# A hybrid decoder layer: chunk levels of gated linear attention by running products of decays on 64x64 quarters, and the gate's product in one fp32r pass

## The chip, the cores and the metric

The kernel runs on one core of a Trainium2 chip. The metric is the device time of one execution in microseconds (us), the median of several. The engines are named as in the profile: PE (TensorE matmuls), PEld (its weight loads, which overlap them), DVE (VectorE), ACT (ScalarE), POOL (GpSimd) and SP (SyncE, which here issues nearly all DMAs).

## The reference

One layer: x (1, 256, 1024) float32; RMSNorm, one input projection, softmax attention with 8 heads of 64 (one block of 256 keys, so plain causal attention per query block of 128), gated linear attention with 4 heads (key width 64, value width 128), an output projection, then a gated feed-forward block with a short convolution. The change touches the gated linear attention alone:

```python
log_a = jax.nn.log_sigmoid((gate_lr @ w_gate_up[l] + b_gate[l]).astype(jnp.float32)) / GLA_GATE_TAU

def gla_attention(q, k, v, log_a):
    """S_t = diag(alpha_t) S_{t-1} + k_t^T v_t ;  o_t = q_t S_t."""
    ...
    qc = to_chunks(q * (dk ** -0.5))
    kc, vc = to_chunks(k), to_chunks(v)
    G = jnp.cumsum(to_chunks(log_a), axis=3)
    ...
        diff = G_[:, :, :, None, :] - G_[:, :, None, :, :]
        decay = jnp.exp(jnp.where(causal[None, None, :, :, None], diff, -jnp.inf))
        A = jnp.einsum('bhtd,bhsd,bhtsd->bhts', q_, k_, decay)
```

So A[t, s] is the sum over d of q[t, d] k[s, d] times the product of the decays of the positions s+1 to t; gate_lr has 16 columns (RANK).

## The kernel before

All matrices stand transposed, 128 features by tokens. Products of the large projections are made in fp32r with both factors split into a high and a low part: `mm3` (L108 to L111) issues three matmuls, high by high, high by low, low by high. ACT makes the high part of each weight piece (`split_hi`, L92), DVE the low part (`split_lo`, L95), half a slot of 2048 columns at a time, ahead of its use; SP loads the next slot when one is free.

The attention runs in 64 steps q (L613 to L659). Steps 0 to 7 project the gated attention's q, k and the gate's 16 columns; 8 to 23 project the softmax heads' q and k (twelve 256-column matmuls a step); 24 to 47 project v, the gated attention's v and its output gate (six 512-column matmuls a step); 48 to 63 are the output projection, and the feed-forward block follows. A table `plan` (L540 to L592) names what else is emitted at the start of each step: `on(q, f)`. PE's order is exactly that of the code. The instructions of ACT and DVE are ordered by a scheduler, with `tc.high_priority()` for the softmax's maxima and exponentials (`m_softmax1`) and for `m_pt`; each engine then works its list in order.

PSUM: four banks `acc` for the projections, and four banks `att`, taken in turn by everything else. A fifth `att` waits until the first is released by its last reader.

The gated attention, before: `g_evac` copies the projection out (step 10), `g_transpose_lr` and `g_transpose` turn it (steps 10, 11), `g_gate_mm` (L297, step 12) multiplies the 16 gate columns in plain float32, which the profile records as two matmuls each; `g_gate` makes the log decay, `g_scan` the running sum Gc over each 128 tokens. The lower triangle of each 128x128 block is then made level by level. For a level with block length b in 32, 16, 8, 4, 2, 1, 64 (`LEVELS`), `lvl_a` subtracts Gc at the pivots and takes exp, `lvl_b` multiplies k and q by it into `kt` and `qt`, `lvl_c` makes the scores on PE, and `lvl_d_` copies the wanted ones under a mask into `ATd` (for 64, a plain copy into `AT`). `qt` holds the two heads of a pair side by side with zeros in the other head's rows, so that a matmul has 128 rows of k, 64 columns of stationary data and 64 moving columns (two heads by 32). The block of tokens 128 to 255 against 0 to 127 comes from `l128_a`, `l128_b`, `l128_c`.

The softmax heads come in pairs pr = 0 to 3: `m_scores(pr)` (step 30, 33, 36, 39) takes two banks, one a head, and multiplies 128 queries by 128 and by 256 keys; `m_softmax1` takes the maxima on DVE (L495) and the exponentials on ACT (L500); `m_pt` turns the weights (L515) and `m_av` multiplies by v (L527, L528). The level matmuls stand at steps 25, 27, 30, 33, 36, 38 and 41, the last block's at 44; in steps 30, 33 and 36 `lvl_c` is emitted right before `m_scores`.

Of the kernel before, what the change touches and what calls it, by code (L numbers as in the profile page):

```python
# [27 lines left out]
LEVELS = [32, 16, 8, 4, 2, 1, 64]  # L28
# [6 lines left out]
def trunk_kernel(ctx: ExitStack, tc: tile.TileContext, xT_d, wG_d, w5_d, wo_d, up_d, dn_d,  # L35
                 par_d, gla_g_d, fin_g_d, wgu_d, cos_d, sin_d, causal_d, lvl_d, ident_d, out_d):
    nc = tc.nc
    V, A, T, DMA = nc.vector, nc.scalar, nc.tensor, nc.sync
# [169 lines left out]
    lrT = at.tile([RANK, S], F32, name="lrT")  # L208
    kts = [at.tile([128, 512], F32, name=f"kt{i}") for i in range(2)]
    qts = [at.tile([128, 4, 2, 64], F32, name=f"qt{i}") for i in range(2)]  # L210
    qt128 = at.tile([128, 2, 2, 128], F32, name="qt128")
    resets = at.tile([128, 512], F32, name="y", bufs=2)
    nc.gpsimd.memset(resets, 1.0)
    nc.gpsimd.memset(resets.rearrange("p (n t) -> p n t", t=128)[:, :, 0:1], 0.0)
    for i in range(2):
        nc.gpsimd.memset(kts[i], 0.0)
        nc.gpsimd.memset(qts[i], 0.0)
    nc.gpsimd.memset(qt128, 0.0)
    nc.gpsimd.memset(AT[64:128, :, 0:64], 0.0)
    mqT = at.tile([128, 4, S], F32, name="mqT")  # L220
# [45 lines left out]

    def g_transpose_lr():
        p = att()
        for tt in range(2):
            T.transpose(p[:RANK, tt * 128:(tt + 1) * 128], gqk[:, tt, 256:272], ident)  # L270
        A.activation(lrT, p[:RANK, :S], AF.Copy)
# [22 lines left out]
    def g_gate_mm():  # L294
        p = att()
        for pr in range(2):
            T.matmul(p[:, pr * S:(pr + 1) * S], wgu[:, pr * 128:(pr + 1) * 128], lrT,  # L297
                     start=True, stop=True)
# [15 lines left out]
    def g_scan():  # L314
        la = at.tile([128, 512], F32, name="d", bufs=2)
        V.tensor_sub(la, st["mn"], st["ln"])
        V.tensor_tensor_scan(Gc, resets, la, 0.0, op0=ALU.mult, op1=ALU.add)

    lv = {}

    def lvl_a(l):
        b = LEVELS[l]
        d = at.tile([128, 512], F32, name="d", bufs=2)
        e = at.tile([128, 512], F32, name="e", bufs=2)
        dv = d.rearrange("p (n two b) -> p n two b", two=2, b=b)
# [4 lines left out]
        V.tensor_sub(dv[:, :, 0, :], pb, gvw[:, :, 0, :])  # L330
        V.tensor_sub(dv[:, :, 1, :], gvw[:, :, 1, :], pb)
        A.activation(e, d, AF.Exp, scale=1.0 / TAU)
        lv[l] = e

    def lvl_b(l):
        b = LEVELS[l]
        e = lv[l]
        kt, qt = kts[l % 2], qts[l % 2]

        def blk(x):  # L340
            return x.rearrange("p (n two b) -> p n two b", two=2, b=b)

        gk_ = gkT.rearrange("p a t -> p (a t)")
        gq_ = gqT.rearrange("p a t -> p (a t)")
        V.tensor_mul(blk(kt)[:, :, 0, :], blk(gk_)[:, :, 0, :], blk(e)[:, :, 0, :])  # L345
        for h in range(2):
            ps = slice(64 * h, 64 * h + 64)
            o = qt[ps, :, h, :].rearrange("p g (n b) -> p g n b", b=b)
            q_ = gq_[ps].rearrange("p (g n two b) -> p g n two b", g=4, two=2, b=b)[:, :, :, 1, :]
            e_ = e[ps].rearrange("p (g n two b) -> p g n two b", g=4, two=2, b=b)[:, :, :, 1, :]  # L350
            V.tensor_mul(o, q_, e_)  # L351

    def lvl_c(l):
        kt, qt = kts[l % 2], qts[l % 2]
        p = att()
        if LEVELS[l] == 64:
            for g in range(4):
                T.matmul(p[0:64, g * 128:(g + 1) * 128], kt[:, g * 128:g * 128 + 64],
                         qt[:, g].rearrange("p h t -> p (h t)"), start=True, stop=True)
        else:  # L360
            for g in range(4):
                for j in range(2):
                    T.matmul(p[64 * j:64 * j + 64, g * 64:(g + 1) * 64],
                             kt[:, g * 128 + 64 * j:g * 128 + 64 * j + 64],
                             qt[:, g, :, 32 * j:32 * j + 32], start=True, stop=True)
        st["lv", l] = p

    def lvl_d_(l):
        b = LEVELS[l]
        p = st["lv", l]  # L370
# [6 lines left out]
        V.copy_predicated(o, m, p[:, :256].rearrange("p (i n b) -> p i n b", i=8, b=b))  # L377
# [5 lines left out]
    def l128_a():  # L383
        d = at.tile([128, 2, 128], F32, name="d", bufs=2)
        e = at.tile([128, 2, 2, 128], F32, name="e", bufs=2)
        G4 = Gc.rearrange("p (a b t) -> p a b t", a=2, b=2)
        V.tensor_sub(d, G4[:, :, 0, 127:128].to_broadcast([128, 2, 128]), G4[:, :, 0, :])
        A.activation(e[:, 0], d, AF.Exp, scale=1.0 / TAU)
        A.activation(e[:, 1], G4[:, :, 1, :], AF.Exp, scale=1.0 / TAU)
        lv["128"] = e  # L390

    def l128_b():
        e = lv["128"]
        kt = kts[1].rearrange("p (a t) -> p a t", a=4)
        V.tensor_mul(kt[:, 0:2], gkT[:, :, 0:128], e[:, 0])
        for h in range(2):
            ps = slice(64 * h, 64 * h + 64)
            V.tensor_mul(qt128[ps, :, h, :], gqT[ps, :, 128:256], e[ps, 1])

    def l128_c():  # L400
        p = att()
        for pr in range(2):
            T.matmul(p[:, pr * 256:(pr + 1) * 256], kts[1][:, pr * 128:(pr + 1) * 128],
                     qt128[:, pr].rearrange("p h t -> p (h t)"), start=True, stop=True)
        A.activation(AT01.rearrange("p a t -> p (a t)"), p, AF.Copy)
# [74 lines left out]
    def m_scores(pr):  # L480

        for hh in range(2):
            st["s", 2 * pr + hh] = att()
        for c0, c1 in ((0, 128), (128, 384)):
            for hh in range(2):
                ps = slice(64 * hh, 64 * hh + 64)
                T.matmul(st["s", 2 * pr + hh][:, c0:c1], mqT[ps, pr, c0:c0 + 128], mkT[ps, pr, 0:c1 - c0],
                         start=True, stop=True)
# [74 lines left out]
    on(14, g_scan)  # L563
    for l in range(7):
        b = 21 + 11 * l // 4
        on(b, lvl_a, l)
        on(b + 1, lvl_b, l)
        on(b + 4, lvl_c, l)
        on(b + 5, lvl_d_, l)
    on(b + 5, lvl_join)  # L570
    on(39, l128_a)
    on(42, l128_b)
    on(44, l128_c)
# [457 lines left out]
```

## Time and profile before

| | us |
|---|---|
| median of three runs | 316.96 (316.83 to 317.05) |
| the profiled execution's own time | 317.14 |
| its span | 315.4 |
| PE busy, share of the span | 97% |
| DVE busy, share | 80% |
| ACT busy, share | 65% |
| granted PE clock, mean | 0.996 |

A busy engine is one that executes an instruction; PE's matmuls are pipelined and their ends are modelled, so what a matmul costs is read from the start of one row to the start of the next, not from its duration. The prediction works with such differences. In the views, `x16` after a group is the number of instruction records in it, and a bracket names the idle time before it and what ended that.

### The profile page before, as it was taken

What the parts mean: (1) busy time and instruction counts of PE and PEld (TensorE: products, weight loads), DVE (VectorE), ACT (ScalarE), POOL (GpSimd) and SP (SyncE); (2) the same over time, 40 slices, a digit from 0 to 9 for tenths busy, and PEclk for the clock granted to TensorE, in tenths of its full rate; (3) what the DMA queues carried; (4) which work ended last, traced back from release to release, by engine and by line L of the source; (5) the groups of instructions that cost most, each with busy time, mean ns of one, the idle gap of its engine ahead of it and who ended that gap; (6) DMA issues with size and microseconds to landing.
All of it is one profiled execution on the core that took longest, in us unless ns stands there. A gap on an engine that the chain in (4) does not pass through costs nothing.

```text
span 315.4 us, 5840 instructions
## 1 busy us (share of the span) xinstructions
PE 306.6 (97%) x2296; PEld 283.1 (90%) x2296; DVE 252.9 (80%) x472; ACT 203.8 (65%) x370; POOL 3.9 (1%) x17
## 2 busy tenths in 40 slices
PE   7899999999999999999999999999999999999992
PEld 6899997776888999999999999999999999999982
DVE  3887999999647677999999988877777777776643
ACT  5878989497858478367676556666665555544362
POOL 4000000000000000000000000000000000000000
PEclk9999999999999999999999999999999999999998
DMA  7999533342361525496555664545555622120003
GB/s 199 374 413 411 201 135 133 133 150 120 135 219 50 178 90 200 157 380 268 200 202 200 225 220 177 195 185 202 201 202 200 262 72 69 67 69 0 2 0 135
DMA packets 12444, 55.40 MB, mean 176 GB/s; under 512 B 1392, under 2 KB 3200, under 8 KB 8064
## 3 DMA queue, kind: packets, MB, share of 16 engines
q1 hardware_dynamic: 12272, 54.76, 47.2%
q8 instruction: 18, 0.29, 0.3%
q10 hardware_dynamic: 144, 0.26, 0.2%
q14 instruction: 10, 0.08, 0.1%
HBM read 53.97 MB, written 1.05 MB: 174 GB/s over the span
## 4 chain that ended last, share of the span: by engine, by line
PE 79%; DVE 9%; ACT 5%; issue 2%; DMA 2%; SPq 1%; DVEq 0%; ACTq 0%
PE att L109 14%; PE att L111 14%; PE att L110 14%; PE acc L110 11%; PE acc L109 10%; PE acc L111 10%; DVE lo L95 2%; DMA xg<-in_xT 2%; ACT qs L466 1%; DVE qt L351 1%; DVE att L495 1%; ACT hi L92 1%; PE att L527 1%; DVE ATd L377 1%; DVE kt L345 1%
## 5 line engine op out<-in xcount | busy, mean ns | idle before, releaser
L92 ACT ACTIVATE hi<-raw 128x1024 fp32r<-128x1024 f32 (+3 forms) x84 | 80.1, 971 | 50.9 <-PE att L110 43.2
L95 DVE TENSOR_TENSOR lo<-raw,hi 128x1024 fp32r<-128x1024 f32 (+3 forms) x86 | 93.7, 1098 | 13.3 <-ACT hi L92 13.2
L109 PE MATMUL att<-hh,hi 128*128 128x256 f32 x352 | 98.5, 280 | 0.0
L111 PE MATMUL att<-hh,lo 128*128 128x256 f32 x352 | 98.4, 279 | 0.0
L110 PE MATMUL att<-hl,hi 128*128 128x256 f32 x352 | 98.3, 279 | 0.0
L109 PEld LDWEIGHTS att<-hh,hi 128*128 128x128 f32 x352 | 66.2, 188 | 0.0
L111 PEld LDWEIGHTS att<-hh,lo 128*128 128x128 f32 x352 | 66.2, 188 | 0.0
L110 PEld LDWEIGHTS att<-hl,hi 128*128 128x128 f32 x352 | 66.2, 188 | 0.0
L757 DVE SCALAR_TENSOR_TENSOR c<-us,par,c 128x256 f32<-128x256 f32 x88 | 40.7, 482 | 4.1 <-ACT c L749 2.5
L749 ACT ACTIVATE c<-us,par 128x256 f32<-128x256 f32 x44 | 24.0, 591 | 21.5 <-DVE us L739 16.0
L111 PE MATMUL acc<-dhi,gl 128*128 128x512 f32 (+1 forms) x88 | 32.3, 367 | 0.0
L110 PE MATMUL acc<-dlo,gh 128*128 128x512 f32 (+1 forms) x88 | 32.2, 366 | 0.0
L109 PE MATMUL acc<-dhi,gh 128*128 128x512 f32 (+1 forms) x88 | 31.8, 361 | 0.0
L696 DVE TENSOR_TENSOR dlo<-draw,dhi 128x1024 fp32r<-128x1024 f32 x22 | 26.6, 1218 | 0.0
L739 DVE TENSOR_TENSOR us<-att,rb 128x512 f32<-128x512 f32 x20 | 13.8, 688 | 15.9 <-PE att L111 15.9
L109 PE MATMUL acc<-hi,ah 128*128 128x512 f32 (+1 forms) x64 | 25.6, 399 | 0.7 <-ACT hi L92 0.7
L110 PE MATMUL acc<-lo,ah 128*128 128x512 f32 (+1 forms) x64 | 24.2, 378 | 0.7 <-DVE lo L95 0.7
L111 PE MATMUL acc<-hi,al 128*128 128x512 f32 (+1 forms) x64 | 23.7, 371 | 0.0
L691 ACT ACTIVATE dhi<-draw 128x1024 fp32r<-128x1024 f32 x22 | 23.1, 1050 | 0.0
L110 PEld LDWEIGHTS acc<-dlo,gh 128*128 128x128 f32 x88 | 16.5, 188 | 3.0
L109 PEld LDWEIGHTS acc<-dhi,gh 128*128 128x128 f32 x88 | 16.6, 188 | 2.9
L111 PEld LDWEIGHTS acc<-dhi,gl 128*128 128x128 f32 x88 | 16.5, 188 | 2.6
(191 smaller groups left out, 528.9 us busy)
## 6 DMA issues: line engine op xcount, KB each, us to landing
raw<-in_up SPq DMA_DIRECT2D x22, 1024.0 KB, 4.8
draw<-in_dn SPq DMA_DIRECT2D x22, 512.0 KB, 5.7
raw<-in_w SPq DMA_DIRECT2D x8, 1024.0 KB, 7.3
raw<-in_wo SPq DMA_DIRECT2D x4, 1024.0 KB, 4.8
raw<-in_w SPq DMA_DIRECT2D x4, 512.0 KB, 8.1
raw<-in_wG SPq DMA_DIRECT2D x2, 528.0 KB, 7.3
raw<-in_wG SPq DMA_DIRECT2D x3, 264.0 KB, 4.0
xg<-in_xT SPq DMA_DIRECT2D x2, 256.0 KB, 6.4
```

Of the source, the lines that this page charges most:

```text
L92: A.activation(self.hi[:, a:b], self.raw[:, a:b], AF.Copy)
L95: V.tensor_sub(self.lo[:, a:b], self.raw[:, a:b], self.hi[:, a:b])
L109: T.matmul(out, sh, mh, start=first, stop=False, **kw)
L110: T.matmul(out, sh, ml, start=False, stop=False, **kw)
L111: T.matmul(out, sl, mh, start=False, stop=last, **kw)
L345: V.tensor_mul(blk(kt)[:, :, 0, :], blk(gk_)[:, :, 0, :], blk(e)[:, :, 0, :])
L351: V.tensor_mul(o, q_, e_)
L691: A.activation(hi, downs[i][0], AF.Copy)
L696: V.tensor_sub(lo, d, hi)
L739: V.tensor_tensor(u[:, :, 2:], upo[i][2].rearrange("p (a t) -> p a t", a=2), rb[:, None, :].to_broadcast([128, 2, S]), op=ALU.mult)
L749: A.activation(cv[i][:, a], u[:, a, 2:], AF.Identity, bias=par[:, P_CB + m:P_CB + m + 1], scale=par[:, P_CW + 2 * 2 * NP + m:P_CW + 2 * 2 ...
L757: V.scalar_tensor_tensor(c[:, a], u[:, a, w:w + S], par[:, wc:wc + 1], c[:, a], op0=ALU.mult, op1=ALU.add)
```

## The change

Three things are edited.

The gate's product: the 16 gate columns are split into high and low parts on DVE (`g_lr_split`) and stacked, so is its weight (`g_wgs`, two small copies on ACT and two subtractions on DVE), and `g_gate_mm` becomes one fp32r matmul with 128 rows for each pair of heads. The weight's load `wgu` moves from step 4 to step 1 in SP's list.

The levels: there is no running sum any more. `g_decay` takes the decay itself, `dec[0] = exp(la)`, and the levels run from small to large, b = 1, 2, 4, 8, 16, 32, each on the result of the one before: `lvl_u` multiplies the second half of each block of q by the running decay, the first half of k by its own, both in place, and multiplies neighbouring decays into a table of half the length. `lvl_c` no longer has zeros: each matmul has 64 rows (one head), 64 stationary and 32 moving columns, one quarter of the array, and the two heads go to two banks. The 64 level and the last 128x128 block are made together in `lvl_last`, also by quarters. What is written in place may not be overwritten before the matmuls of the level before have read it, so `lvl_u(l)` waits for the burst of level l-1.

The places: levels 0 and 1 go in one burst at step 24; levels 2 to 5 are emitted inside `m_scores`, in columns 384 to 511 of the two score banks, at steps 30, 33, 36 and 40 (the last pair was at 39), and the scores themselves are cut into quarters. `lvl_last` stands at step 44, its copies at 45. The fourth `m_av` moves from step 47 to 48.

```diff
-LEVELS = [32, 16, 8, 4, 2, 1, 64]
+LEVELS = [1, 2, 4, 8, 16, 32]
...
+    def g_wgs():
+        with tc.high_priority():
+            for i in range(2):
+                A.activation(wgs[32 * i:32 * i + RANK], wgu, AF.Copy)
+            for i in range(2, 4):
+                V.tensor_sub(wgs[32 * i:32 * i + RANK], wgu, wgs[0:RANK])
+
+    def g_lr_split():
+        with tc.high_priority():
+            lr = gqk[:, :, None, 256:272].to_broadcast([128, 2, 2, RANK])
+            l4 = lrs.rearrange("p a (n two z) r -> p a n two z r", two=2, z=2)[:, :, :, :, 0]
+            V.tensor_copy(l4[:, :, :, 0], lr)
+            V.tensor_sub(l4[:, :, :, 1], lr, l4[:, :, :, 0])
...
     def g_gate_mm():
         p = att()
         for pr in range(2):
-            T.matmul(p[:, pr * S:(pr + 1) * S], wgu[:, pr * 128:(pr + 1) * 128], lrT,
+            T.matmul(p[:, pr * S:(pr + 1) * S], wgs[:, pr * 128:(pr + 1) * 128], lrT,
                      start=True, stop=True)
...
-        V.tensor_tensor_scan(Gc, resets, la, 0.0, op0=ALU.mult, op1=ALU.add)
+        A.activation(dec[0], la, AF.Exp, scale=1.0 / TAU)
...
+    def lvl_u(l):
...
+        V.tensor_mul(two(gqf, c)[:, :, 1], q, dc[:, :, 0].to_broadcast([128, n, c]))
+        V.tensor_mul(two(gkf, c)[:, :, 0], two(gkf, c)[:, :, 0], dc[:, :, 1].to_broadcast([128, n, c]))
+        V.tensor_mul(dec[l], dc[:, :, 0, 0], dc[:, :, 1, 0])
...
+    def lvl_c(l, p, c):
         b = LEVELS[l]
...
+        for g in range(4):
+            for j in range(2):
+                for h in range(2):
+                    ps = slice(64 * h, 64 * h + 64)
+                    a = g * 128 + 64 * j
+                    q = q1[ps, a // 2:a // 2 + 32] if l == 0 else two(gqf[ps, a:a + 64], b)[:, :, 1]
+                    k = gk1.rearrange("p a t -> p (a t)") if l == 0 else gkf
+                    T.matmul(p[h][64 * j:64 * j + 64, c + 32 * g:c + 32 * g + 32], k[ps, a:a + 64], q,
+                             start=True, stop=True)
...
+    def lvl_last():
+
+        p = [att() for _ in range(2)]
+        for g in range(4):
+            for h in range(2):
+                ps = slice(64 * h, 64 * h + 64)
+                T.matmul(p[h][0:64, g * 64:(g + 1) * 64], gkf[ps, g * 128:g * 128 + 64],
+                         gqf[ps, g * 128 + 64:(g + 1) * 128], start=True, stop=True)
+        for pr in range(2):
+            for t, q in enumerate((gqT[:, pr, 128:192], q128[:, pr])):
+                for j, k in enumerate((k128[:, pr], gkT[:, pr, 64:128])):
+                    for h in range(2):
+                        ps = slice(64 * h, 64 * h + 64)
+                        c = 256 + pr * 128 + 64 * t
+                        T.matmul(p[h][64 * j:64 * j + 64, c:c + 64], k[ps], q[ps], start=True, stop=True)
...
     def m_scores(pr):
 
+        p = [att() for _ in range(2)]
+        lvl_c(pr + 2, p, 384)
+        for c0, c1 in ((0, 128), (128, 384)):
+            for j in range(2):
+                for hh in range(2):
+                    ps = slice(64 * hh, 64 * hh + 64)
+                    a = c0 + 64 * j
+                    T.matmul(p[hh][64 * j:64 * j + 64, c0:c1], mqT[ps, pr, a:a + 64], mkT[ps, pr, 0:c1 - c0],
+                             start=True, stop=True)
...
     for h in range(HM):
-        b = 30 + 3 * h // 2
+        b = (30, 33, 36, 40)[h // 2] + h % 2
         if h % 2 == 0:
             on(b, m_scores, h // 2)
+            on(b + 1, lvl_d_, 2 + h // 2)
...
+            on(b + 2, *((lvl_u, 3 + h // 2) if h < 6 else (lvl_u64,)))
```

Where the instructions stand now is shown at three places.

PE at step 36, where the third pair of softmax heads gets its scores. Before, with L363 as `lvl_c`, L487 as `m_scores` and L109 to L111 as the first product of the projection behind it:

```order
L363 MATMUL att<-qt_130,kt_128 64x64 x8
L487 MATMUL att<-mkT,mqT 128x128 x2
L487 MATMUL att<-mkT,mqT 128x256 x2
L109 MATMUL acc<-hi,ah 128x512
L110 MATMUL acc<-lo,ah 128x512
L111 MATMUL acc<-hi,al 128x512
```

Now, on PE at the same step, with L377 as `lvl_c` and L506 as `m_scores`:

```order
L377 MATMUL att<-gqT,gkT 64x32 x16
L506 MATMUL att<-mkT,mqT 64x128 x4
L506 MATMUL att<-mkT,mqT 64x256 x4
L109 MATMUL acc<-hi,ah 128x512
L110 MATMUL acc<-lo,ah 128x512
L111 MATMUL acc<-hi,al 128x512
```

The order of the three groups is kept, with twice the matmuls of half the width; the level's matmuls had a bank of their own and now go alternately to the two banks of the scores.

DVE ahead of the maxima of heads 2 and 3 (the pair of step 33). Before, with L508 and L506 of the softmax of heads 0 and 1, L345 and L351 as `lvl_b`, L377 as `lvl_d_` and L495 as the first maximum:

```order
L508 TENSOR_SCALAR pe<-pe,mx 128x256
L345 TENSOR_TENSOR kt_128<-gkT,e 128x128x2
L351 TENSOR_TENSOR qt_130<-gqT,e 64x4x64 x2
L506 RECIPROCAL mx<-mx 128x2
L377 COPY_PREDICATED ATd<-lvl,att 128x64x4
L495 ISA att,mx<-att,causal 128x128
```

Now, on DVE ahead of the same maxima, with L527 and L529 of the softmax of head 1, L352 and L353 as `lvl_u`, L388 as `lvl_d_` and L516 as the first maximum:

```order
L527 RECIPROCAL mx<-mx 128x2
L529 TENSOR_SCALAR pe<-pe,mx 128x256
L352 TENSOR_TENSOR gqT<-gqT,dec_128 128x32x8
L353 TENSOR_TENSOR gkT<-gkT,dec_128 128x32x8
L388 COPY_PREDICATED ATd<-lvl,att 128x4x4x8 x2
L516 ISA att,mx<-att,causal 128x128
```

Two products stand where three stood, two masked copies of half the size where one stood, and the whole softmax of head 1 is now ahead of them.

DVE behind those maxima, up to the two scalings L497 that ACT's exponentials of head 2 and of head 3 wait for. Before (L95 is a low part of a weight, L330 and L331 are `lvl_a`):

```order
L495 ISA mx 128x1
L497 TENSOR_SCALAR mx<-mx 128x2
L508 TENSOR_SCALAR pe<-pe,mx 128x256
L497 TENSOR_SCALAR mx<-mx 128x2
L95 TENSOR_TENSOR lo<-raw,hi 128x1024
L330 TENSOR_TENSOR d<-Gc 128x256
L331 TENSOR_TENSOR d<-Gc 128x256
L506 RECIPROCAL mx<-mx 128x2 x2
```

Now, on DVE at the same place, with L518 as the scaling:

```order
L516 ISA mx 128x1
L518 TENSOR_SCALAR mx<-mx 128x2
L95 TENSOR_TENSOR lo<-raw,hi 128x1024
L518 TENSOR_SCALAR mx<-mx 128x2
L527 RECIPROCAL mx<-mx 128x2
L95 TENSOR_TENSOR lo<-raw,hi 128x1024
L529 TENSOR_SCALAR pe<-pe,mx 128x256
```

A low part of 1024 columns now stands between the scaling of head 2 and that of head 3, where a short scaling of weights stood.

More of the change, by code (lines that the diff above doesn't have):

```diff
@@ L207, in trunk_kernel @@
     AT01 = at.tile([128, 4, 128], F32, name="AT01")
[L208 to L218, printed above, removed]
+    wgs = at.tile([128, 256], F32R, name="wgs")
+    lrs = at.tile([128, 2, 8, RANK], F32R, name="lrs")
+    lrT = at.tile([128, S], F32R, name="lrT")
     nc.gpsimd.memset(AT[64:128, :, 0:64], 0.0)
+    nc.gpsimd.memset(wgs.bitcast(F32), 0.0)
+    nc.gpsimd.memset(lrs.bitcast(F32), 0.0)
     mqT = at.tile([128, 4, S], F32, name="mqT")
@@ L280, in g_transpose @@
         A.activation(dst.rearrange("p a t -> p (a t)"), p, AF.Copy, scale=sc)
+        if which:
+            A.activation(gk1.rearrange("p a t -> p (a t)"), p, AF.Copy)
     def g_diag():
@@ L335, in lvl_b @@
-    def lvl_b(l):
-        b = LEVELS[l]
[L337 to L366, printed above, removed]
+        A.activation(dec[0], la, AF.Exp, scale=1.0 / TAU)
@@ L379, in lvl_join, with lvl_first @@
+    def lvl_first():
+        p = [att() for _ in range(2)]
+        for l in range(2):
+            lvl_c(l, p, 128 * l)
     def lvl_join():
@@ L381, in lvl_join, with lvl_last_d @@
         A.activation(AT[0:64, :, 0:64], ATd[0:64], AF.Copy)
[L383 to L395, printed above, removed]
-        for h in range(2):
[L397 to L405, printed above, removed]
+    def lvl_last():
[8 more added lines that the diff above has]
+                for j, k in enumerate((k128[:, pr], gkT[:, pr, 64:128])):
+                    for h in range(2):
+                        ps = slice(64 * h, 64 * h + 64)
+                        c = 256 + pr * 128 + 64 * t
+                        T.matmul(p[h][64 * j:64 * j + 64, c:c + 64], k[ps], q[ps], start=True, stop=True)
+        st["last"] = p
+    def lvl_last_d():
+        for h in range(2):
+            p = st["last"][h]
+            A.activation(AT.rearrange("p (g h) t -> p g h t", h=2)[0:64, :, h, 64:128],
+                         p[0:64, 0:256].rearrange("p (g t) -> p g t", g=4), AF.Copy)
+            A.activation(AT01.rearrange("p (a h) t -> p a h t", h=2)[:, :, h],
+                         p[:, 256:512].rearrange("p (a t) -> p a t", a=2), AF.Copy)
     def gv_evac(tt):
@@ L480, in m_scores @@
     def m_scores(pr):
-        for hh in range(2):
[L483 to L488, printed above, removed]
+        p = [att() for _ in range(2)]
+        lvl_c(pr + 2, p, 384)
[6 more added lines that the diff above has]
+                             start=True, stop=True)
+        for hh in range(2):
+            st["s", 2 * pr + hh] = p[hh]
     def m_softmax1(h):
@@ L562, in trunk_kernel @@
     on(12, g_gate)
[L563 to L573, printed above, removed]
+    on(14, g_decay)
+    on(15, lvl_u, 0)
+    on(19, lvl_u, 1)
+    on(24, lvl_first)
+    on(25, lvl_d_, 0)
+    on(25, lvl_d_, 1)
+    on(26, lvl_u, 2)
     for tt in range(2):
```

68 lines of the change are left out of this document (42 added, 26 removed).

## The prediction, made before the changed kernel ran

> **What bounds the kernel now.** I read first the page's busy times, then what PE waited for, then stretches of 20 us through the attention.
>
> ```profile
> PE 306.6 (97%) x2296; PEld 283.1 (90%) x2296; DVE 252.9 (80%) x472; ACT 203.8 (65%) x370; POOL 3.9 (1%) x17
> PE att L527 <- ACT pe L500: 0.6, 1, 0.6
> 40.00:60.00 20.00, 20.00 (x152) 16.41 (x152) 19.83 (x42) 14.06 (x22) 0.00 (x0) 1.00 0.42 154
> 60.00:80.00 20.00, 19.42 (x147) 14.21 (x146) 19.85 (x65) 17.78 (x48) 0.00 (x0) 1.00 0.34 113
> ```
>
> PE sets the time: it is busy in all of 40 to 60 us, and from 60 to 80 it lacks only 0.58, the one wait behind the start, on an exponential of ACT. But DVE (the fourth column) is just as full: 19.83 and 19.85 of 20. So what PE saves before 80 us counts only as far as DVE's list lets PE run ahead; what it saves behind counts in full, since after 80 us DVE has air and PE waits for nothing. The granted clock is 1.00 throughout and no term comes from it.
>
> **The change part by part.**
>
> *The gate's product.* PE's order of time at step 12, and ACT's copy of the turned gate columns:
>
> ```profile
> 23.55 0.37 ACT L271 ACTIVATE lrT<-att 16x256 f32<-16x256 f32 x1 [0.18 <-PE att L270]
> ...
> 26.91 0.28 PE L111 MATMUL acc<-ah,lo 128*128 128x256 f32 x1
> 27.12 1.13 PE L297 MATMUL att<-lrT,wgu 16*128 16x256 f32 x4
> 28.18 0.39 PE L109 MATMUL acc<-ah,hi 128*128 128x256 f32 x1
> 28.41 0.28 PE L110 MATMUL acc<-al,hi 128*128 128x256 f32 x1
> 28.52 0.28 PE L111 MATMUL acc<-ah,lo 128*128 128x256 f32 x1
> ```
>
> An fp32r product of 256 columns costs 0.12 (28.41 to 28.52). The plain float32 product takes from 27.03 (26.91 and 0.12) to 28.29 (28.41 less 0.12), the slower L109 behind it counted: 1.26. Two fp32r products take 0.24: **1.02 saved**. The two turns ahead of it only move. The extra small products on DVE and copies on ACT lie before and in gaps of both engines: the turned gate columns were ready at 23.92, 3.2 before their use, and the longer path, with its turn a step (1.4) later, takes some 1.5 of that. Without this cover the splitting would cost about its length, 0.5.
>
> *The bursts.* PE at steps 36, 38 (the wait), 41 and 44:
>
> ```profile
> 67.83 0.69 PE L363 MATMUL att<-qt,kt 128*64 128x64 f32 x16
> 68.45 0.93 PE L487 MATMUL att<-mkT,mqT 64*128 64x128 f32 x8
> 69.31 0.50 PE L109 MATMUL acc<-hi,ah 128*128 128x512 f32 x1
> 69.64 0.40 PE L110 MATMUL acc<-lo,ah 128*128 128x512 f32 x1
> ...
> 73.89 0.66 PE L527 MATMUL att<-pt,mv 128*64 128x256 f32 x4 [0.58 <-ACT pe L500]
> ...
> 80.74 1.09 PE L358 MATMUL att<-qt,kt 128*64 128x128 f32 x8
> 81.66 0.65 PE L527 MATMUL att<-pt,mv 128*64 128x256 f32 x4
> ...
> 87.37 1.03 PE L403 MATMUL att<-qt,kt 128*128 128x256 f32 x4
> 88.33 0.65 PE L527 MATMUL att<-pt,mv 128*64 128x256 f32 x3
> ```
>
> and, from the start, the row with the least to stream:
>
> ```profile
> 19.44 0.50 PE L248 MATMUL att<-ones,s 128*128 128x1 f32 x4
> 19.80 0.36 PE L109 MATMUL acc<-ah,hi 128*128 128x256 f32 x1
> ```
>
> From start to start a level costs 0.62, the scores 0.86, the 64 level 0.92, the last block 0.96, and each return to 512-column work makes its first matmul 0.10 longer (69.31 to 69.64 against the usual 0.23). L358 shows records of 128 columns one after another: 0.92 for 8, 0.115 each. L363's 16 records of 64 columns would need as much, 0.92, and took 0.62: its two halves of the columns run abreast, in 8 steps of about 0.058, with some 0.15 for entering and leaving. L487 (four records of 128 and four of 256 columns, by L403 0.22 each) would need 1.3 alone and took 0.86: its two halves of the rows run abreast.
>
> The new matmuls are quarters, halves in both. If four run abreast, a level's 32 records are 8 steps. How long is a step of 32 columns? L248 has one moving column and still takes 0.36 for 4 records, 0.11 at the later ones: its weights, 128 columns wide, set that. Half the width is 0.055, so the weights alone keep a step near 0.058 although there is half as much to stream. Bounds for a level's streaming: 0.25 (by columns) to 0.46 (by weights) to 0.93 (one record after another or two abreast); I take 0.46, since L248 is the nearest row. A level by itself then gains nothing; what goes is changes between shapes.
> - Levels 0 and 1: two bursts of 0.62 and 0.10 become one of 0.93, 0.15 and 0.10: 0.25 saved.
> - Steps 30, 33, 36: 1.48 becomes 0.46, 0.66 (scores as before) and 0.15, some 1.28: 0.2 saved each.
> - Fourth pair: 0.62, 0.86 and 0.10 become 1.37: 0.2 saved.
> - 64 level and last block: 0.92 and 0.96 become 8 steps of pairs and 8 of fours, 0.93, and 0.1: 0.85 saved.
>
> On the skill, apart from the sum: the Trainium skill, TensorEngine Tiling (Array Packing), section Instruction Overhead, says each matmul carries about 60 cycles of overhead, so one should not take a tiling factor from a dimension that is small already. It speaks against cutting 64 moving columns to 32. L248 agrees (one column is not cheap), and by this rule the sum is as above: the levels gain nothing.
>
> PE's own sum is 1.02, 0.25, 0.6, 0.2 and 0.85, that is 2.9, and 0.58 if the old wait goes: 3.5.
>
> *DVE and ACT.* Grouped rows of DVE from 20 to 100 us:
>
> ```profile
> L351 DVE TENSOR_TENSOR qt<-gqT,e 64x256 f32<-64x256 f32 x14 | 5.8, 415 | 0.1
> L377 DVE COPY_PREDICATED ATd<-lvl,att 128x256 f32<-128x256 int32 x6 | 3.2, 536 | 0.1
> L345 DVE TENSOR_TENSOR kt<-gkT,e 128x256 f32<-128x256 f32 x7 | 3.0, 426 | 0.0
> L330 DVE TENSOR_TENSOR d<-Gc 128x256 f32<-128x256 f32 x7 | 2.9, 419 | 0.0
> L331 DVE TENSOR_TENSOR d<-Gc 128x256 f32<-128x256 f32 x7 | 2.9, 419 | 0.0
> L317 DVE TENSOR_TENSOR_SCAN Gc<-y,d 128x512 f32<-128x512 f32 x1 | 1.2, 1226 | 0.1
> ```
>
> Out go 15.8 (L351, L345, L330, L331, L317). In come 15 products of 256 elements at 0.42, 6.3, and small ones, about 1.5; the masked copies become 12 of half size, between 0.27 (half of 536) and 0.54 each, so 0 to 3.2 more; I take 0.5. DVE is freed of some 7 us, mostly before step 30 and around the softmax. PE's small gain would be hidden by none of this if the softmax chain moved forward by as much. There I see **a new wait**, at step 36.
>
> The bursts' banks: four `att` in turn. In the old step 36 the level used the first bank of heads 2 and 3, and the scores asked for the second 0.62 later. Now the first two matmuls of the burst go to both, so the burst starts only when head 3's exponentials have ended.
>
> ```profile
> 62.50 0.35 DVE L508 TENSOR_SCALAR pe<-pe,mx 128x256 f32<-128x256 f32 x1
> ...
> 64.36 0.29 DVE L495 CUSTOM_DVE_ANT_0 att<-att,causal 128x128 f32<-128x128 f32 x1
> ...
> 65.58 0.17 DVE L497 TENSOR_SCALAR mx<-mx 128x2 f32<-128x2 f32 x1
> 65.65 0.35 DVE L508 TENSOR_SCALAR pe<-pe,mx 128x256 f32<-128x256 f32 x1
> 65.92 0.17 DVE L497 TENSOR_SCALAR mx<-mx 128x2 f32<-128x2 f32 x1
> 66.00 1.22 DVE L95 TENSOR_TENSOR lo<-raw,hi 128x1024 fp32r<-128x1024 f32 x1
> 66.59 0.49 ACT L517 ACTIVATE pt<-att 128x384 f32<-128x384 f32 x1
> 66.96 0.38 ACT L500 ACTIVATE pe<-att,mx 128x128 f32<-128x128 f32 x1
> 67.31 0.49 ACT L500 ACTIVATE pe<-att,mx 128x256 f32<-128x256 f32 x1
> ```
>
> They ended at 67.80. PE would now come to step 36 at 67.83 less 1.02, 0.25 and twice 0.2: 66.2. DVE's list ahead of the maxima shrinks from 1.86 (62.50 to 64.36) to about 1.5, two products and two masked copies behind the scaling of head 1, so they start 0.3 to 1.0 earlier. But between the two scalings of `mx` now stands a low part (1.14, from 66.00 to the next row) where L508 took 0.27. Head 3's scaling is done between 65.9 and 66.6; ACT then needs an exponential, a copy from PSUM and an exponential, 1.2. The bank is free at 67.1 to 67.8: PE waits 0.9 to 1.6, I take 1.2, and its burst starts at 67.4, only **0.4 earlier** than before. Everything saved up to here beyond 0.4 is given back, however large. PE waits in order, so the projection behind it waits too.
>
> From there: the burst 0.2; the old wait of 0.58 shrinks to about 0.2, as the first to ask for head 4's bank is now `m_pt`, 0.8 behind `m_av`, while DVE again has a low part ahead of these maxima: 0.4; fourth pair 0.2; the last block 0.85. The fourth `m_av` now stands right ahead of the output projection, whose tenth matmul needs its result; ACT's list puts the first silu before that copy. Rows of before:
>
> ```profile
> 94.91 0.47 PE L109 MATMUL acc<-hi,ah 128*128 128x512 f32 x1
> ...
> 96.69 0.21 ACT L178 ACTIVATE sm<-sm 128x4 f32<-128x4 f32 x1
> 97.81 1.28 ACT L411 ACT_TABLE_LOAD   x1
> 99.11 1.27 ACT L411 ACTIVATE gr<-acc,rsx 128x512 f32<-128x512 f32 x2
> ```
>
> On the old clock: ACT is free at 96.90, has the table at 98.2, the first silu (about 0.6) at 98.8, the copy at 99.3, and DVE's low part follows at 99.9. PE leaves the gated attention's last products at 94.9, does two steps (3.0), `m_av` (0.8) and nine matmuls (1.1) and asks at 99.9 too. A wait of 0 to 0.5; I take 0.1. SP's and POOL's lists change by one place of a 16 KB load and some memsets, hidden behind the weights' loads: 0.
>
> **The sum:** 0.4, 0.2, 0.4, 0.2 and 0.85, less 0.1: 1.95 from the profiled execution's 317.14, so 315.2. That execution lies 0.18 above the median of 316.96, which gives **315.0**.
>
> **The rivals.**
> - *No new wait.* The softmax chain keeps up, or DVE's freed 7 us bring it forward by 1.2 more. For it: those 7 us; against: the extra low part. The whole 3.5 come: 313.5, and with steps set by the 32 columns, up to 1.3 less for the levels: 312.2. 15%.
> - *A floor per record.* L363's row reads as well as 16 records of 0.029 as 8 pairs of 0.058. If records cannot start faster, a level takes 0.93, the last burst 0.46 more. PE then comes to step 36 four times 0.47 later, at 68.1, and waits for nothing: 0.25 lost there, 0.27 at its burst, 0.58 gained, 0.26 lost, 0.39 gained: 0.2 saved, 316.8. 11%. The Trainium skill, TensorE: Matmul & The Clock Gate, Part 1, states such a floor, about 25 ns from start to start; its Part 3 has tiles start some 4 ns apart, by which the floor does not hold between quarters. No trace here has quarters, so neither is borne out.
> - *Slower: quarters run only two abreast.* Rows show halves of the columns abreast, and halves of the rows, never both. Then a level is 0.93, scores 1.3 instead of 0.66, the last burst 0.46 more: six times 0.47, four times 0.66 and 0.46, 5.9 more on PE against the 3.5: 2.4 slower, 319.4. It turns slower once the bursts grow by over 3.5 in all. 8%.
> - *A larger wait.* The masked copies at 0.54 each and the products that wait for one another push the chain at step 36 back by 1 to 1.5 more, and step 48 waits 0.5: 316.5. 11%.
>
> **How the numbers follow.** The forecast has 55%, from 314.2 to 316.0 (the wait 0.4 to 2 at step 36). No change means within 0.2%, 316.33 to 317.59, about what a measurement of this kernel can tell. Faster: the forecast, the first rival and a part of the larger wait, 0.73; the same: the floor and the rest, 0.17; slower: 0.10. The range leaves out the slower rival, the upper end of the larger wait and the lower end of the first rival: 312.8 to 317.2.
>
> **What would show it.** The gate's two matmuls starting 0.12 apart. Step 36: the level's 32 records in 0.46 and a wait of PE for ACT of about 1.2 ahead of L377, with head 3's last exponential ending just before. Steps 30 and 33 of 1.28 without a wait. A step of fours at 0.03, 0.06 or 0.11 decides between the rivals on PE. It would be wrong if the wait stood elsewhere or were missing, or if PE's path behind step 48 waited anew.

## The result, and the profile after

| | before | after |
|---|---|---|
| median time, us | 316.89 (four runs) | 314.28 (314.16 to 314.64, four runs) |
| ratio, 95% interval | | 0.9919 (0.9902 to 0.9937) |
| the profiled execution's own time | 317.14 | 314.39 |
| its span | 315.4 | 311.8 |
| time less span | 1.74 | 2.59 |
| granted PE clock, mean | 0.996 | 0.998 |

The kernel is 2.6 us faster, where 1.95 were forecast. The time less the span needs attention: in the two profiled executions the span, from the first instruction to the last, fell by 3.6, and the time by 2.75 only. Over all executions shown here the median span is 315.1 before and 311.75 after (3.35 less), and what lies outside it 1.79 (1.73 to 1.84) before and 2.5 (2.34 to 2.59) after.

The page's busy times of the changed kernel, then PE's waits (us in total, how often, the longest), then the two stretches of 20 us of the attention (length, then the busy time of PE, PEld, DVE, ACT and POOL with their records, the granted clock, and the share and GB/s of the DMA engines):

```profile
PE 304.9 (98%) x2458; PEld 282.9 (91%) x2458; DVE 246.0 (79%) x464; ACT 201.5 (65%) x367; POOL 1.8 (1%) x12
```

```profile
PE att L73 <- DVE warm L70: 1.0, 1, 1.0
PE acc L109 <- ACT hi L92: 0.2, 1, 0.2
```

```profile
40.00:60.00 20.00, 20.00 (x244) 16.44 (x245) 18.54 (x40) 13.75 (x22) 0.00 (x0) 1.00 0.53 192
60.00:80.00 20.00, 20.00 (x199) 14.40 (x192) 16.74 (x62) 17.10 (x44) 0.10 (x1) 1.00 0.34 126
```

The list has no wait of PE between the first loads and the end: neither the old one of 0.58 nor the predicted one of 1.2 is there. DVE, which was full in both stretches, has 1.5 and 3.3 us of air. Its masked copies, as a group from 20 to 100 us (the last numbers are busy time and the mean of one in ns):

```profile
L388 DVE COPY_PREDICATED ATd<-lvl,att 128x128 f32<-128x128 int32 x12 | 3.3, 359 | 0.0
```

PE's order of time at steps 12, 24, 36 and 44 and at the old wait's place:

```profile
26.67 0.28 PE L111 MATMUL acc<-ah,lo 128*128 128x256 f32 x1
26.79 0.40 PE L311 MATMUL att<-lrT,wgs 128*128 128x256 f32 x2
27.03 0.28 PE L109 MATMUL acc<-ah,hi 128*128 128x256 f32 x1
...
43.91 0.67 PE L377 MATMUL att<-q,gk 64*64 64x32 f32 x32
44.40 0.65 PE L377 MATMUL att<-gqT,gkT 64*64 64x32 f32 x32
44.98 0.50 PE L109 MATMUL acc<-hi,ah 128*128 128x512 f32 x1
...
65.58 0.67 PE L377 MATMUL att<-gqT,gkT 64*64 64x32 f32 x32
66.07 0.86 PE L506 MATMUL att<-mkT,mqT 64*64 64x128 f32 x16
66.86 0.50 PE L109 MATMUL acc<-hi,ah 128*128 128x512 f32 x1
...
70.18 0.66 PE L548 MATMUL att<-pt,mv 128*64 128x256 f32 x4
...
84.46 0.62 PE L405 MATMUL att<-gqT,gkT 64*64 64x64 f32 x14
...
85.54 0.50 PE L109 MATMUL acc<-hi,ah 128*128 128x512 f32 x1
```

From start to start: the gate's product 0.24, a level 0.49, a level with its scores 1.28 (65.58 to 66.86), levels 0 and 1 together 1.07, the last burst 1.08. No row carries a bracket. At step 36 the burst starts at 65.58; the first maximum of heads 2 and 3 on DVE, and ACT's list up to that moment (L538 copies turned weights, of head 0 and then of head 1; L521 is the exponentials):

```profile
62.45 0.29 DVE L516 CUSTOM_DVE_ANT_0 att<-att,causal 128x128 f32<-128x128 f32 x1
...
63.81 0.50 ACT L538 ACTIVATE pt<-att 128x384 f32<-128x384 f32 x1
...
64.52 0.50 ACT L521 ACTIVATE pe<-att,mx 128x256 f32<-128x256 f32 x1
...
65.49 0.48 ACT L538 ACTIVATE pt<-att 128x384 f32<-128x384 f32 x1
65.86 0.48 ACT L521 ACTIVATE pe<-att,mx 128x256 f32<-128x256 f32 x1
```

The second exponential of head 2 ends at 65.02; that of head 3 only starts at 65.86, when PE's burst has been under way for 0.28. So the burst cannot be using head 3's bank. Nor can it use the bank of head 1's turned weights, which are copied until 65.97. Of the four banks two are left: head 2's, and the one from which head 0's turned weights had been copied by 64.31.

### The profile page after: what moved, and what is told of

The parts are those of the page before. It is cut to its first block, busy times and chain, and to the rows that moved or that the text cites. A ratio compares the mean times of both kernels' runs of the same rounds, so it can differ in the third digit from the quotient of the medians.

```text
span 311.8 us, 6135 instructions
## 1 busy us (share of the span) xinstructions
PE 304.9 (98%) x2458; PEld 282.9 (91%) x2458; DVE 246.0 (79%) x464; ACT 201.5 (65%) x367; POOL 1.8 (1%) x12
## 4 chain that ended last, share of the span: by engine, by line
PE 96%; DMA 1%; ACT 1%; DVE 0%; SPq 0%; issue 0%; DVEq 0%; ACTq 0%
PE acc L109 15%; PE acc L110 15%; PE acc L111 15%; PE att L110 15%; PE att L109 15%; PE att L111 15%; DMA xg<-in_xT 1%; PE att L377 1%; PE att L536 1%; PE att L506 1%; PE att L548 1%; PE att L439 1%; PE acc L816 0%; PE att L437 0%; PE att L470 0%; PE att L549 0%
## 5 line engine op out<-in xcount | busy, mean ns | idle before, releaser
L95 DVE TENSOR_TENSOR lo<-raw,hi 128x1024 fp32r<-128x1024 f32 (+3 forms) x86 | 93.6, 1099 | 12.6 <-ACT hi L92 12.5
L109 PE MATMUL att<-hh,hi 128*128 128x256 f32 x352 | 98.5, 280 | 0.0
L111 PE MATMUL att<-hh,lo 128*128 128x256 f32 x352 | 98.4, 279 | 0.0
L109 PEld LDWEIGHTS att<-hh,hi 128*128 128x128 f32 x352 | 66.2, 188 | 0.0
L111 PEld LDWEIGHTS att<-hh,lo 128*128 128x128 f32 x352 | 66.2, 188 | 0.0
L111 PE MATMUL acc<-dhi,gl 128*128 128x512 f32 (+1 forms) x88 | 32.3, 367 | 0.0
L109 PE MATMUL acc<-dhi,gh 128*128 128x512 f32 (+1 forms) x88 | 31.8, 361 | 0.0
L109 PE MATMUL acc<-hi,ah 128*128 128x512 f32 (+1 forms) x64 | 25.6, 400 | 0.2 <-ACT hi L92 0.2
L111 PE MATMUL acc<-hi,al 128*128 128x512 f32 (+1 forms) x64 | 24.2, 378 | 0.0
L109 PEld LDWEIGHTS acc<-dhi,gh 128*128 128x128 f32 x88 | 16.6, 188 | 2.9
L111 PEld LDWEIGHTS acc<-dhi,gl 128*128 128x128 f32 x88 | 16.5, 188 | 2.6
```

The source lines that it names most:

```text
L95: V.tensor_sub(self.lo[:, a:b], self.raw[:, a:b], self.hi[:, a:b])
L109: T.matmul(out, sh, mh, start=first, stop=False, **kw)
L111: T.matmul(out, sl, mh, start=False, stop=last, **kw)
```

## The experiments

What the runs had to settle: why the predicted wait is missing, what each part of the change is worth by itself, what sets the price of a quarter, and what lies outside the span. Each experiment was run beside the kernel before, whose median was 316.9 each time. "Outside" is the time less the span.

### Which bank the burst gets (e1, e5)

```diff
-        return ps_att.tile([128, 512], F32, name="att")
+        i = turn[0] % 4
+        turn[0] += 1
+        return ps_att.tile([128, 512], F32, name=f"att{i}")
```

> The changed kernel, but the four banks `att` are handed out strictly in turn, as the prediction assumed. In its own trace the burst of step 36 starts at 65.58 us without a wait, while head 3's last exponential runs to 66.34. Theory 1 (the wait is missing only because the pool gives the burst other banks than head 3's): now the burst waits for that exponential, starts at about 66.4, PE shows a wait of about 0.8 us for ACT ahead of it, and as PE waits for nothing behind, the time is about 0.8 more: 315.1. Theory 2 (the softmax chain is early enough whatever the bank, since DVE is freed of 7 us): no wait, 314.3.

It took 318.96 us, ratio 1.0064 (1.0052 to 1.0076), and did not answer the question: strictly in turn, the gate's product at step 12 got the bank of the row turn, which DVE reads late. PE's row there, and windows of the granted clock (the column behind POOL's) after it:

```profile
29.80 0.47 PE L319 MATMUL att<-lrT,wgs 128*128 128x256 f32 x2 [2.78 <-DVE sin L265]
```

```profile
30.00:32.00 2.00, 2.00 (x15) 2.00 (x15) 1.97 (x4) 1.10 (x3) 0.00 (x0) 0.78 0.78 298
32.00:34.00 2.00, 2.00 (x12) 2.00 (x11) 2.00 (x4) 1.97 (x6) 0.00 (x0) 0.50 0.75 297
34.00:36.00 2.00, 2.00 (x17) 2.00 (x16) 1.11 (x4) 1.57 (x6) 0.00 (x0) 0.86 0.34 63
```

PE lost 2.8 in the wait and another 1.7 because its clock fell to a half afterwards (0.22, 0.50 and 0.14 of 2 us each). So late a PE finds a wait of only 0.2 at step 36. The second attempt keeps the first banks as the changed kernel has them; the three engines' lists are the same as there:

```diff
+    first = [0, 1, 2, 3, 0, 3, 1, 2, 3, 1, 2, 0, 3, 1, 2]
+    order = [0, 3, 1, 2]
...
+            i = first[n] if n < len(first) else order[(n - len(first)) % 4]
```

> The changed kernel with its own banks `att` up to the scores of heads 2 and 3, and from there on the four banks strictly in turn; the first attempt (e1) had put the wait elsewhere, at the gate's product. The burst of step 36 now gets the banks of heads 2 and 3. Theory 1 (only the pool's free choice removed the predicted wait): the burst waits for head 3's last exponential, which ended at 66.34 in the changed kernel, so it starts near 66.4 instead of 65.58, PE shows a wait of 0.8 us for ACT there, and the span grows by about 0.8 from 311.7 to 312.5. Theory 2 (the chain of the softmax is early enough): no wait, 311.7. For the time outside the span: 2.3 to 2.6 as in the changed kernel if it belongs to the kernel's instructions, 1.9 as in e1 if it hangs on the banks' names.

315.16 us, ratio 0.9942 (0.993 to 0.9955), median span 312.7. PE and then ACT around step 36:

```profile
65.55 0.30 PE L389 MATMUL att<-gqT,gkT 64*64 64x32 f32 x2
66.44 0.60 PE L389 MATMUL att<-gqT,gkT 64*64 64x32 f32 x27 [0.59 <-ACT pe L533]
...
67.71 0.50 PE L121 MATMUL acc<-hi,ah 128*128 128x512 f32 x1
```

```profile
65.82 0.48 ACT L533 ACTIVATE pe<-att,mx 128x256 f32<-128x256 f32 x1
```

The first quarter (two records) goes to head 2's bank and starts; the second wants head 3's and stands until its exponential has ended. The burst takes 2.16 instead of 1.28, the time is 0.88 more: theory 1. A wait at the predicted place is real once the banks are those of heads 2 and 3, and the pool's choice of bank is what removed it.

### The two halves of the change by themselves (e2, e3, e7)

> The kernel before with the gate's product alone changed (split, stacked, one fp32r pass). On PE the product takes 0.24 us instead of 1.26. Theory 1 (the terms add): 1.0 less, 315.9. Theory 2 (DVE's full list from 40 to 80 us gives it back: PE comes 1.0 earlier and the old wait of 0.58 on head 4's side at 73.89 grows by as much): within 0.3 of the kernel before, 316.6 to 316.9, and PE's wait for ACT at 72 to 74 us is 1.3 to 1.6 us.

> The changed kernel with the gate's product as it was before (plain float32, 16 rows); levels, scores and last block as changed. Theory 1 (the terms add, PE waits nowhere in the changed kernel): 1.0 more than the changed kernel, 315.3. Theory 2 (it is the freed DVE that lets the rest move forward, and the gate's gain would be given back before): within 0.3 of the changed kernel, 314.3 to 314.6. The time that lies outside the span (1.74 us before, 2.3 to 2.6 after the change): by whichever of e2 and e3 shows over 2.2, that edit brought it.

| | time, us | ratio to before | median span | outside |
|---|---|---|---|---|
| gate alone (e2) | 319.54 | 1.0081 (1.0066 to 1.0095) | 317.75 | 1.81 |
| levels alone (e3) | 314.82 | 0.9942 (0.9923 to 0.996) | 312.9 | 1.95 |
| both | 314.28 | 0.9919 (0.9902 to 0.9937) | 311.75 | 2.5 |

On top of the levels the gate's product takes 1.15 off the span, near its 1.02 on PE: theory 1 of e3, by the span. The times differ by 0.54 only, between the two theories, since 0.55 more lies outside the span with both edits. Neither e2 (1.81) nor e3 (1.95) shows the 2.5 there, so neither edit brings it by itself. Alone the gate's product makes the kernel 2.65 us slower, which neither theory had. PE's waits in e2, and DVE's list ahead of the longest:

```profile
PE att L381 <- DVE qt L369: 2.3, 1, 2.3
...
PE att L533 <- ACT pe L525: 0.7, 1, 0.7
```

```profile
58.77 1.23 DVE L95 TENSOR_TENSOR lo<-raw,hi 128x1024 fp32r<-128x1024 f32 x1
59.91 0.43 DVE L395 COPY_PREDICATED ATd<-lvl,att 128x256 f32<-128x256 int32 x1
...
60.91 0.42 DVE L363 TENSOR_TENSOR kt<-gkT,e 128x256 f32<-128x256 f32 x1
61.25 0.85 DVE L369 TENSOR_TENSOR qt<-gqT,e 64x256 f32<-64x256 f32 x2
```

```profile
62.00:64.00 2.00, 1.76 (x24) 1.10 (x24) 1.97 (x5) 2.00 (x4) 0.00 (x0) 0.84 0.00 0
64.00:66.00 2.00, 2.00 (x7) 1.60 (x6) 1.88 (x12) 0.86 (x2) 0.00 (x0) 0.50 0.65 201
66.00:68.00 2.00, 2.00 (x10) 1.54 (x9) 1.97 (x6) 1.00 (x5) 0.00 (x0) 0.81 0.77 324
```

DVE is full, and the scheduler's new order puts the operands of the level of step 33 behind a low part and other work; PE, 1.0 early, finds them missing, stands 2.33, and then again runs at a granted 0.50. Is it that order alone? In e7 the level of step 33 comes first, by this line in `lvl_a` and `lvl_b`:

```diff
+        with (tc.high_priority() if l == 3 else nullcontext()):
```

> The kernel before with the gate's product alone changed, as e2, and the differences, exponentials and products of the level of step 33 given high priority on DVE and ACT. In e2 PE waited 2.3 us there for `qt`, whose products stood behind a low part and the maxima. Theory 1 (only that order took the gain): the wait is gone and the time is 1.0 below the kernel before, 315.9. Theory 2 (DVE's list is full and something else is late instead): another wait of 1 to 2.5 us, at step 36 or at the next turn of softmax weights, and 316.9 to 319.

318.1 us, ratio 1.0043 (1.0028 to 1.0059). PE's waits:

```profile
PE att L535 <- ACT pe L527: 0.7, 2, 0.5
PE att L383 <- DVE qt L371: 0.6, 1, 0.6
PE att L535 <- DVE pe L528: 0.6, 1, 0.6
```

Theory 2: four shorter waits, 1.9 in all, have taken the place of the long one. In both orders that were tried, DVE with the old levels had no room for a PE that is earlier. The kernel before shows why in the chain of work that ended last: from 28 to 73.9 us it runs through DVE and ACT alone, and PE takes it over at the end of the old wait:

```profile
73.29 0.34 DVE d L331
73.89 0.66 PE att L527 x4
```

So by this chain DVE and ACT set the time up to there, and not PE, as busy as PE was. In the same stretch of the changed kernel, and of e3, the chain holds PE alone: with the new levels DVE is off it, and there the gate's product counts.

### What a quarter costs (e4, e8, e6)

```diff
+        if l == 2:
+            every.sort(key=lambda x: x[1])
+        if l == 3:
+            every.sort(key=lambda x: x[2])
+        if l == 4:
+            every.sort(key=lambda x: (x[1], x[2]))
```

> The changed kernel with the 32 quarters of a level in another order at three steps, the products unchanged: at step 30 only the two halves of the rows alternate, at step 33 only the two halves of the columns, at step 36 eight quarters in the same place follow one another. Theory 1 (four quarters run abreast because they lie in four places; one place takes 0.058 a record): 0.93 us at steps 30 and 33 instead of 0.49, 1.86 at step 36; some 2.2 us more in all, 316.5. Theory 2 (records simply start about 0.015 apart wherever they lie): 0.49 at all three, 314.3. Theory 3 (one kind of halves alone is enough to run four abreast): 0.49 at one of steps 30 and 33, 0.93 at the other.

One time, 315.31. PE at steps 30 and 36:

```profile
53.43 0.75 PE L384 MATMUL att<-gqT,gkT 64*64 64x32 f32 x26
53.97 0.33 PE L513 MATMUL att<-mkT,mqT 64*64 64x128 f32 x2
...
54.13 0.22 PE L384 MATMUL att<-gqT,gkT 64*64 64x32 f32 x1
...
54.96 0.50 PE L109 MATMUL acc<-hi,ah 128*128 128x512 f32 x1
...
65.94 1.25 PE L384 MATMUL att<-gqT,gkT 64*64 64x32 f32 x29
...
67.97 0.50 PE L109 MATMUL acc<-hi,ah 128*128 128x512 f32 x1
```

The bursts take 1.53 (step 30; the same at 33) and 2.03 (step 36) instead of 1.28. That the order counts rules theory 2 out, and rows and columns alone cost the same, which rules out theory 3. Theory 1 is right in kind and too high in price (0.25 and 0.75 more, not 0.44 and 1.37): records for a free place start ahead of those that still wait for a busy one, as the first scores do at 53.97, ahead of the last level records at 54.13.

```diff
+                    if l in (2, 3):
+                        q, o = q[:, :16 // b], o[:, :16]
```

> The changed kernel with 16 instead of 32 moving columns in the level matmuls of steps 30 and 33 (half of the queries of these two levels are left out, and so are their masked copies). Theory 1 (the weight load of 64 columns sets a step of four quarters): the steps stay at 0.058 and the level at 0.49 us, as at step 36 of the same run. Theory 2 (the moving columns set it): 0.03 a step and 0.27 a level. Theory 3 (a fixed time per record of about 0.0145): 0.49 as well; e4, where a record in the same place took 0.058, speaks against it.

One time, 313.9. PE at steps 30 and 36:

```profile
53.50 0.66 PE L380 MATMUL att<-gqT,gkT 64*64 64x16 f32 x32
53.99 0.86 PE L511 MATMUL att<-mkT,mqT 64*64 64x128 f32 x16
...
65.52 0.67 PE L380 MATMUL att<-gqT,gkT 64*64 64x32 f32 x32
66.00 0.86 PE L511 MATMUL att<-mkT,mqT 64*64 64x128 f32 x16
```

0.49 and 0.48: half the columns save nothing. Theory 2 is out. That it is the weight load was not tried with narrower weights; the runs show only that each place takes its eight records in 0.49, with 16 or 32 columns.

```diff
-                T.matmul(p[h][0:64, g * 64:(g + 1) * 64], gkf[ps, g * 128:g * 128 + 64],
+                j = g % 2
+                T.matmul(p[h][64 * j:64 * j + 64, g // 2 * 64:g // 2 * 64 + 64], gkf[ps, g * 128:g * 128 + 64],
```

> The changed kernel with the eight matmuls of the 64 level in `lvl_last` spread over both halves of the columns, so that four instead of two run abreast; ACT then copies four pieces of half the length instead of two. Theory 1 (abreast is set by the place): four steps of two become two steps of four, 0.115 each, so the burst of step 44 takes 0.85 us instead of 1.08 and the time falls by 0.2, to 314.1, since PE waits for nothing behind. Theory 2 (ACT's two extra copies, or something else, hold up the products behind it): no gain, 314.3, with a wait of PE on ACT at step 46.

```profile
84.29 0.46 PE L406 MATMUL att<-gqT,gkT 64*64 64x64 f32 x16
...
85.14 0.50 PE L109 MATMUL acc<-hi,ah 128*128 128x512 f32 x1
```

The burst takes 0.85 instead of 1.08, as in theory 1. But the time fell by 0.94 to **313.34**, ratio 0.9888 (0.9874 to 0.9901), the fastest of all kernels here: its median span is 0.2 below that of the changed kernel, and the time outside it is 1.77 instead of 2.5.

### What lies outside the span (e9 to e12)

```diff
+    scr = const.tile([128, 2], F32, name="scr")
+    for i in range(2):
+        A.activation(scr[:, i:i + 1], eps, AF.Copy)
```

> The changed kernel with two ACT copies of 128x1 added ahead of its first activation, where ACT waits for the first load from 2 to 3.3 us; all else is in the same order. What is tested is the time outside the span: 2.3 to 2.6 us in the changed kernel, e4, e5 and e8, whose traces each hold 439 ACT instructions, and 1.7 to 2.0 in the kernel before (450), e1 (440 instructions, with one execution of 2.5), e2 (450), e3 (438), e6 (441) and e7 (449). Theory 1 (it hangs on the number of ACT's instructions, whatever they do): 441 as in e6, 1.8 outside, the same span of 311.7, and a time of 313.5, 0.7 below the changed kernel. Theory 2 (it hangs on something else, for instance on what e6's copies do): 2.5 outside and 314.3.

> As e9, with two DVE copies of 128x1 instead of the ACT ones, ahead of DVE's first subtraction, where DVE waits too. Theory 1 (ACT's number, 439 as before): 2.5 outside the span, 314.3. Theory 2 (any change of the program's length moves it): 1.8 outside, 313.5.

> e3 (the levels alone, 438 ACT instructions, 1.9 to 2.0 us outside the span, 314.82) with one ACT copy of 128x1 added ahead of ACT's first activation: 439. Theory 1 (the number of ACT's instructions): 2.3 to 2.6 outside the span, 312.8 of span as in e3, 315.3: slower by 0.5 through one instruction that nothing waits for. Theory 2: no change, 314.8.

> e11 held no more ACT instructions than e3 (438 in the trace of each: the added copy took the place of a separate instruction that waits). So e3 with two such copies, 439 in the trace as in the changed kernel. Theory 1 (the number of ACT's instructions sets the time outside the span): 2.3 to 2.6 us there, the span of 312.8 as in e3 and e11, and 315.2 to 315.4. Theory 2 (ACT's number alone is not it, DVE's or the rest of the program counts too; e10 with two more DVE copies had 2.1): 1.9 to 2.0 and 314.7 to 314.8.

| | ACT / DVE instructions in the trace, waits and DMA issues counted | time, us | ratio to before | median span | outside |
|---|---|---|---|---|---|
| changed kernel | 439 / 569 | 314.28 | 0.9919 (0.9902 to 0.9937) | 311.75 | 2.34 to 2.59 |
| e9 | 441 / 569 | 313.63 | 0.9897 (0.9884 to 0.9911) | 311.85 | 1.75 to 1.80 |
| e10 | 439 / 571 | 314.11 | 0.9909 (0.9895 to 0.9922) | 312.0 | 2.08 to 2.13 |
| levels alone (e3) | 438 / 564 | 314.82 | 0.9942 (0.9923 to 0.996) | 312.9 | 1.90 to 2.02 |
| e11 | 438 / 564 | 314.71 | 0.9931 (0.9917 to 0.9944) | 312.8 | 1.90 to 1.98 |
| e12 | 439 / 564 | 314.76 | 0.9928 (0.9912 to 0.9944) | 312.65 | 2.08 to 2.16 |

e9 is clear: two copies that nothing reads and nothing waits for, with the span unchanged, take 0.7 off what lies outside it. So the 0.7 belongs neither to the levels nor to the gate as computation. But the number of ACT's instructions alone is not the rule: 439 gives 2.5, 2.1 and 2.1 in three programs, and DVE's copies help by half as much. e11 tested nothing, since its count did not change. Nor does the program fix it in every execution: one of e1's five had 2.51, the others 1.86 to 1.96. The 2.5 is not a slip of the changed kernel's own runs, since e5 and e8, with its numbers of instructions, have 2.14 to 2.48 and 2.40. What the chip does in that time stays open.

## Why the prediction came out

315.0 was forecast, with 312.8 to 317.2, and 314.28 measured: inside the range, on the side and near the size given. Point by point it was less good. The points use a table of how far the changed kernel's PE is ahead, by the start of the same row L109 (a first matmul of a projection) in both traces:

| row L109 behind | before, us | after, us | after is ahead by |
|---|---|---|---|
| the first steps | 19.80 | 19.55 | 0.24 |
| the gate's product | 29.70 | 28.43 | 1.27 |
| step 23 | 44.89 | 43.48 | 1.41 |
| levels 0 and 1 | 51.78 | 49.98 | 1.80 |
| step 36 | 70.11 | 67.66 | 2.45 |
| the fourth pair, the old wait before it | 79.94 | 76.89 | 3.05 |
| the 64 level and the last block | 91.61 | 88.09 | 3.52 |
| the fourth `m_av`, step 48 | 100.20 | 96.83 | 3.37 |

- **The gate's product**: 1.02, right (0.24 on PE, 1.15 of span in e3 against both).
- **The bursts**: right by their own rows, less so in what they gave. From start to start levels 0 and 1 saved 0.27 (two of 0.62 and one return of 0.10, less 1.07; 0.25 forecast), steps 30, 33 and 36 0.2 each (0.2), the fourth pair 0.3 (0.2), the 64 level and the last block 0.8 (0.85). A step of fours is 0.058, as the prediction took from L248. The Trainium skill's rule in TensorEngine Tiling (Array Packing), section Instruction Overhead, not to cut a dimension that is small already, fits: with 16 columns as with 32 a level takes 0.49. But a burst also changes the rows beside it, which the forecast left out: by the table levels 0 and 1 gave 0.39, the fourth pair 0.02 (0.60 less the old wait of 0.58), the 64 level and the last block 0.47. One place where the rest went shows in the rows: the turned weights right ahead of a burst of quarters take 0.48 (74.33 to 74.81, 83.98 to 84.46), where the same turns took 0.24 and 0.30 before (78.92 to 79.16, 89.14 to 89.44).
- **DVE freed of 7**: right, 252.9 to 246.0, 6.9. The masked copies are 12 of 0.36, nearer the lower bound. What the prediction had less right is that PE sets the time: up to 73.9 us that holds for its busy share only, while the chain ran through DVE and ACT, so freeing DVE is what let PE's savings count there (e2 and e3).
- **The new wait at step 36**: this step failed, and in two places. The first is its sentence "The bursts' banks: four `att` in turn", as the account of the kernel before has it too. The pool did not hand them out in turn: in the program as built, the burst gets the bank from which the turned weights of head 0 had been copied and the bank of head 2. With the premise made true, e5, PE waits where it was said and for whom. The second is the chain: the maxima of heads 2 and 3 start at 62.45, 1.9 earlier than before (64.36) and not 0.3 to 1.0, and head 3's exponential ended at 66.34, not at 67.1 to 67.8. So in e5 the burst goes on at 66.44 instead of 67.4, and the wait costs 0.88 instead of 1.2. That the time of e5, 315.16, lies next to the forecast of 315.0 is luck.
- **The old wait** was to shrink to 0.2; it is gone.
- **Step 48** waits a little, as forecast (0.1). PE needs the low part of the fourth `m_av` (`ml`), which DVE ends at 96.43:

```profile
96.33 0.28 PE L109 MATMUL acc<-mh,hi 128*128 128x256 f32 x1
96.49 0.39 PE L110 MATMUL acc<-ml,hi 128*128 128x256 f32 x1
```

From 96.33 to the next L109 at 96.83 it is 0.50 against the usual 0.35; a loss of 0.15 that the list of waits does not have.

- **The sum**: 1.95 was forecast; the median span shows 3.35, near PE's own sum of 3.5. Inside the span the first rival came true, "no new wait", which had 15% and 313.5. That its size fits so well is in part chance: the table adds up to 3.37 with 0.24 that was there ahead of the gate's product and 0.14 that came between 29.7 and 44.9 us, in rows that are the same in both kernels; no run shows the cause of either. Then 0.7 that no step had, outside the span, brought 314.28. Two errors of opposite sign (1.5 for the waits, 0.7 outside) left the total closer than its parts; its nearness is luck.
- **The other rivals**: the floor of 0.029 a record and the quarters two abreast are refuted by the 0.49 of a level, 0.015 from one record to the next. So the 25 ns from start to start of the Trainium skill, TensorE: Matmul & The Clock Gate, Part 1, do not hold between quarters. The larger wait did not occur. That DVE's full list can turn PE's gain into a loss was weighed only as a limit; e2 and e7 show it as a price, 2.65 and 1.2 us for the gate alone.

## What to carry to other kernels

Before a wait on a shared buffer goes into a sum, find out which buffer the pool really hands out, since four buffers need not be used in turn. A saving on the busiest engine is worth its size only if the engine that feeds it has room, and the chain that ended last shows which of the two sets the time: the same 1.0 us gained 1.15 of span with the levels changed and cost 1.2 to 2.65 of time without. Compare the spans as well as the times, or a loss outside the span hides a gain inside it.

## What was unexpected on the chip

- **A pause of 2.3 to 2.8 us was followed by half of PE's clock**: 0.84, 0.50, 0.81 in the three stretches of 2 us in e2 and 0.78, 0.50, 0.86 in e1, some 1.7 us lost on top of the pause, which is 3.4 us at half clock each time; after the pause of 0.59 in e5 the granted clock stays at 1.00. The Trainium skill, TensorE: Matmul & The Clock Gate, Part 1, has the clock fall to half after an idle window of about 3.4 us; the half agrees, but here less idle time was enough, and the measurement decides.
- **Matmuls in different quarters do not start strictly in the program's order** (e4, 53.97 against 54.13), so a bad order costs less than places counted one by one.
- **Two idle copies made the kernel 0.65 us faster** (e9 against the changed kernel), all of it outside the span, for a reason that no trace here shows.
